# Matrix product with layer norm: a bank filled in another order, gamma and beta loaded at another place, their second copies cut finer

## The chip, the cores and the metric

The kernel runs on one core of a Trainium2 chip. TensorE multiplies matrices into PSUM, which has eight banks of 128 x 512 fp32 values; VectorE (DVE) and ScalarE (ACT) cast, copy and normalise; GpSimd (POOL) helps at the end; SyncE (SP) computes nothing and issues the DMA transfers between device memory and SBUF. The metric is the time on the device in microseconds, lower is better, as the median of several runs.

## The reference

```python
m, k, n = 2048, 2048, 2048          # all fp32, eps = 1e-5
x = np.matmul(a, b)
mean = np.mean(x, axis=-1, keepdims=True)
var = np.var(x, axis=-1, keepdims=True)
normalized = (x - mean) / np.sqrt(var + eps)
return (gamma * normalized + beta).astype(np.float32)
```

## The kernel before

Both matrices are cast to fp16 and multiplied with fp32 sums. The 2048 rows of `a` are 16 tiles of 128 rows; the inner dimension is 16 k-tiles of 128; the columns are four quarters of 512, one PSUM bank each. A tile's product is four quarters of 16 matmuls.

The first four tiles are worked on together while `b` comes in, k-tile by k-tile: the left half of the columns for k-tiles 0 to 3, the right half for k-tiles 0 to 7, then the rest. These products take seven banks, and the eighth serves the transposes of `a` on TensorE. The eighth product of each pass, the late bank, can only begin when the last transposes have been copied out of it. The right pass reads:

```python
early, late = right[:-1], right[-1]
for g, q in early:
    bank(g, q)
turns = {(1, 6): K1, (2, 4): K1 + 1, (3, 1): K1 + 2, (3, 5): K1 + 3}   # K1, K2 = 4, 8
for t in range(K1):
    if 0 < t < K1 - 1:
        cast_right(t + 1)              # half on VectorE, half on ScalarE
    for j, (g, q) in enumerate(early):
        mm(g, q, t, 0, K2)
        if (t, j) in turns:
            n = turns[t, j]
            turn_first(n)              # four transposes into the eighth bank
            keep_first(n)              # VectorE copies them out
            if n < 2 * K1 - 1:
                cast_first(n + 1)
cast_right(K1)
bank(*late)
for t in range(K1):
    mm(*late, t, 0, K2)
for t in range(K1, K2 - 1):
    cast_right(t + 1)
    for g, q in early:
        mm(g, q, t, 0, K2)
# ... the eighth k-tile, and the copies out of the banks ...
```

From tile 4 on the tiles of `a` are loaded in pieces of 64 KB (twenty transfers for a tile, in two halves), cast by ScalarE and transposed by VectorE. A tile's load, its cast, its transposes and its products are in different steps of the program:

```python
for t in range(K2, n_kt):
    load_b(t, 1)
for h in (0, 1):
    load_tile(4, h)                    # p_0 and p_1 in the profile
for h in (0, 1):
    load_tile(5, h)
# ... the products of the first four tiles ...
new_at(5)
for h in (0, 1):
    load_tile(6, h)
nc.sync.dma_start(gamma_b, gamma.unsqueeze(0).to_broadcast([P, N]))
nc.sync.dma_start(beta_b, beta.unsqueeze(0).to_broadcast([P, N]))
for c in range(4):
    if c % 2 == 0:
        cast_tile(5, c // 2)
        load_tile(7, c // 2)
    transpose_part(5, c)

for i in range(G, last):               # tiles 4 to 14
    if i > G:
        normalise(i - 1)
    if i == last - 2:
        load_halves()
    # ...
    for q in range(n_nb):
        bank(i, q)                     # eight banks in turn: tile 6 takes those of tile 4
        for t in range(n_kt):
            mm(i, q, t)
        stats(i, q)
        if i + 2 < n_mt:
            if q % 2 == 0:
                cast_tile(i + 2, q // 2)
                if i + 4 < n_mt:
                    load_tile(i + 4, q // 2)
            transpose_part(i + 2, q)
        # ...
        if q == 3 and i < 3 * G:
            normalise((i - G) // 2, (i - G) % 2)   # half of one of the first four tiles
```

`normalise` works on VectorE. Its first step for a quarter, `centre`, reads the bank, subtracts the mean and multiplies by `gamma_b`, and so frees the bank; its second, `scale`, multiplies by the inverse deviation and adds `beta_b`; then SyncE stores a half of the tile.

```python
def centre(i, q, u):
    nc.vector.scalar_tensor_tensor(
        u, x_of[i, q], mv_of[i][:, 0:1], gamma_b[:, ds(q * NB, NB)],
        AluOp.subtract, AluOp.mult)

def scale(i, q, u, c):
    nc.vector.scalar_tensor_tensor(
        c[:, ds(q % 2 * NB, NB)], u, rs_of[i], beta_b[:, ds(q * NB, NB)],
        AluOp.mult, AluOp.add)
```

The last tile is worked on as two blocks of 64 rows, each with its left columns on partitions 0 to 63 and its right columns on 64 to 127. It needs gamma and beta laid out in the same way, the second copies:

```python
def load_halves():
    for name, v in (("g", gamma), ("b", beta)):
        gb2[name] = bigp.tile([P, NH], FP32, tag="big", name=f"{name}2")
        for c in (0, 1):
            nc.sync.dma_start(
                gb2[name][ds(HR * c, HR), :],          # HR = 64, NH = 1024
                v[ds(c * NH, NH)].unsqueeze(0).to_broadcast([HR, NH]))
```

Every transfer reports its landing on one of eight semaphores, which are taken in turn (0 to 7), and waits for the transfer that had the same semaphore before it. The last four stores, of the second block of 64 rows, are issued by SyncE and ScalarE, two each.

Of the kernel before, what the change touches and what calls it, by code (L numbers as in the profile page):

```python
# [15 lines left out]
def kernel(  # L16
# [19 lines left out]
    nc = tc.nc  # L36
    P = 128
    M, K = a.shape
    _, N = b.shape
# [4 lines left out]
    NH = N // 2  # L44
# [15 lines left out]
    gamma_b = konst.tile([P, N], FP32)  # L60
    beta_b = konst.tile([P, N], FP32)
# [27 lines left out]
    def cast_right(kt, copies=(nc.vector.tensor_copy, nc.scalar.copy)):  # L89
        w = b_in.pop((kt, 1))  # L90
        for half, copy in enumerate(copies):
            copy(b16[:, kt, 1, ds(PAD + half * NB, NB)], w[:, ts(half, NB)])
# [17 lines left out]
    def cast_first(n):  # L110
        h = first16.tile([P, 4 * P], FP16, tag="h", name=f"h{n}")
        copy = nc.scalar.copy if n in (1, 3, 6, 7) else nc.vector.tensor_copy
        copy(h, a_in[n])
        a_in[n] = h

    def turn_first(n):
        t_of[n] = psum.tile([P, 4, P], FP16, tag="c_ps", bufs=8, name=f"t_ps{n}")
        if n >= 4:
            by_t = a_in[n].rearrange("m (p t) -> m t p", t=4)
        for j in range(4):  # L120
            if n < 4:
                by_t = a_in[n][:, ts(j // 2, 2 * P)].rearrange("m (p t) -> m t p", t=2)
            nc.tensor.transpose(t_of[n][:, j, :], by_t[:, j if n >= 4 else j % 2, :], ident)

    def keep_first(n):
        if n >= 4:
            g, c = pieces[n]
            nc.vector.tensor_copy(at[g][:, ds(4 * c, 4), :], t_of[n])
        else:
            g, e = 2 * (n % 2), n // 2  # L130
            nc.vector.tensor_copy(at[g][:, ts(e, 2), :], t_of[n][:, 0:2, :])  # L131
            nc.vector.tensor_copy(at[g + 1][:, ts(e, 2), :], t_of[n][:, 2:4, :])

    def load_tile(i, h):
        f = firstp.tile([P, 2, 4, P], FP32, tag="first", name=f"p{i}_{h}")
        for c in (0, 1):
            for q in range(4):
                to = f[ds(32 * q, 32), c]
                if h == 0 and c == 0:
                    for e in (0, 1):  # L140
                        nc.sync.dma_start(  # L141
                            to[:, :, ts(e, 64)], a_pieces0[q, e][:, ds(4 * i, 4)])
                else:
                    nc.sync.dma_start(to, a_pieces[q, 2 * h + c][:, ds(4 * i, 4)])  # L144
        tile_in[i, h] = f
# [21 lines left out]
    def bank(i, q):  # L167
        x_of[i, q] = psum.tile([P, NB], FP32, tag="c_ps", bufs=8, name=f"ps_{i}_{q}")

    def mm(i, q, kt, lo=0, hi=n_kt):  # L170
        nc.tensor.matmul(  # L171
            x_of[i, q], at[i][:, kt, :], b16[:, kt, q // 2, ds(PAD + q % 2 * NB, NB)],
            start=(kt == lo), stop=(kt == hi - 1),
        )
# [68 lines left out]
    HR = P // 2  # L243
    gb2, mean_parts = {}, {}
# [14 lines left out]
    def load_halves():  # L259
        for name, v in (("g", gamma), ("b", beta)):  # L260
            gb2[name] = bigp.tile([P, NH], FP32, tag="big", name=f"{name}2")
            for c in (0, 1):
                nc.sync.dma_start(
                    gb2[name][ds(HR * c, HR), :],
                    v[ds(c * NH, NH)].unsqueeze(0).to_broadcast([HR, NH]))

    def halves(name, lo, w):
        return gb2[name][:, ds(lo, w)]
# [131 lines left out]
    with tc.manual_schedule(engines=order):  # L400
# [13 lines left out]
        K1, K2 = 4, 8  # L414
# [19 lines left out]
            load_b(t, 1)  # L434
        for h in (0, 1):
            load_tile(4, h)
        for h in (0, 1):
            load_tile(5, h)

# [2 lines left out]
        early, late = left[:-1], left[-1]  # L442
# [52 lines left out]
        early, late = right[:-1], right[-1]  # L495
# [3 lines left out]
# [5 lines that stand above are left out]
                if (t, j) in turns:  # L504
                    n = turns[t, j]
                    turn_first(n)
                    keep_first(n)
                    if n < 2 * K1 - 1:
                        cast_first(n + 1)
        cast_right(K1)  # L510
        bank(*late)
        for t in range(K1):
            mm(*late, t, 0, K2)
        for t in range(K1, K2 - 1):
            cast_right(t + 1)
            for g, q in early:
                mm(g, q, t, 0, K2)
        for j, (g, q) in enumerate(early):
            mm(g, q, K2 - 1, 0, K2)
# [10 lines left out]
        early, late = left[:-1], left[-1]  # L530
        for g, q in early:
            bank(g, q)
        for t in range(K1, n_kt - 3):
            n = K1 + t
# [48 lines left out]
        new_at(5)  # L583
        for h in (0, 1):
            load_tile(6, h)
        nc.sync.dma_start(gamma_b, gamma.unsqueeze(0).to_broadcast([P, N]))
        nc.sync.dma_start(beta_b, beta.unsqueeze(0).to_broadcast([P, N]))
        for c in range(4):
            if c % 2 == 0:
                cast_tile(5, c // 2)  # L590
# [3 lines left out]
        for i in range(G, last):  # L594
            if i == 6:
                junk = xpool.tile([P, 2 * NB], FP16, tag="x_sb", name="junk")
# [4 lines that stand above are left out]
            if i == last - 1:  # L601
                mean_b()
            if i + 2 < n_mt:
                new_at(i + 2)
            for q in range(n_nb):
                bank(i, q)
# [9 lines that stand above are left out]
                if 6 <= i < 14:  # L616
                    sum_b(4 * (i - 6) + q, junk)
                if q == 3 and i < 3 * G:
                    normalise((i - G) // 2, (i - G) % 2)
# [33 lines left out]
```

## Time and profile before

| | before |
|---|---|
| time, median of 3 runs | 242.94 us (242.8 to 243.04) |
| span of the profiled execution | 242.0 us |
| TensorE busy | 232.4 us, 96% |
| VectorE busy | 196.2 us, 81% |
| ScalarE busy | 97.2 us, 40% |
| mean granted TensorE clock | 0.994 |
| moved by DMA | 53.71 MB, mean 222 GB/s |
| gamma_b, beta_b: issue to landing | 4.5 us, 7.3 us |

All times within the span are in microseconds from its first instruction. A line of a timeline has the start, the duration, the engine, the line of the kernel (L and a number), the operation, what it writes and what it reads, the shapes and the number of instructions merged; in brackets how long the engine stood idle before it and what ended that. A line of a list of waits has who waited for whom, the microseconds in total, how often, and the longest. SPq is SyncE's queue of DMA issues; the duration of an issue is that of the issuing instruction, not of the transfer. PEld is TensorE's load of weights. The numbers behind names only tell tiles of the same name apart: `at_708`, `at_819` and `at_874` are the transposed tiles 4, 5 and 6, and `p_0_216` and `p_1_229` are the two halves of tile 5, `p_0_820` and `p_1_833` those of tile 6, `p_0_846` the first half of tile 7.

### The profile page before, as it was taken

The numbers are of one execution on the slowest core, as the hardware profiler recorded it, in microseconds if no ns is written. First come the engines' busy times: TensorE is split into PE (matmuls) and PEld (weight loads), VectorE is DVE, ScalarE is ACT, GpSimd is POOL, SyncE is SP. The second block draws the span as 40 slices with busy tenths as digits, with TensorE's granted clock in tenths as the row PEclk, the third lists the DMA queues.
The fourth block names the chain that finished last, engine by engine and source line by source line (L and its number), as shares of the span: only waits on it lengthen the run. The fifth ranks groups of instructions, "written<-read, shape, count | busy, mean of one in ns | idle before, by whom it ended". The sixth has DMA issues, their size and how long they took to land.

```text
span 242.0 us, 3619 instructions
## 1 busy us (share of the span) xinstructions
PE 232.4 (96%) x1232; PEld 109.6 (45%) x1232; DVE 196.2 (81%) x377; ACT 97.2 (40%) x159; POOL 6.3 (3%) x10
## 2 busy tenths in 40 slices
PE   8999999999999999999999999999999999999970
PEld 2444455444444444444444444444444444444660
DVE  1476286588679477999999999999999999975882
ACT  3365353464112240219165645637190927301211
POOL 0000000000000000000000000000000000001241
PEclk9999999999999999999999999999999999999997
DMA  6999999994425385448475665648474847980433
GB/s 202 352 405 407 400 402 404 405 412 125 132 65 129 106 307 171 111 106 303 113 257 153 224 192 187 231 126 299 122 294 104 289 120 263 349 260 0 175 86 88
DMA packets 47569, 53.71 MB, mean 222 GB/s; under 512 B 17600, under 2 KB 37184, under 8 KB 47296
## 3 DMA queue, kind: packets, MB, share of 16 engines
q1 hardware_dynamic: 47392, 53.24, 65.4%
q10 hardware_dynamic: 160, 0.26, 0.3%
q8 instruction: 9, 0.15, 0.3%
q14 instruction: 8, 0.07, 0.1%
HBM read 36.70 MB, written 16.78 MB: 221 GB/s over the span
## 4 chain that ended last, share of the span: by engine, by line
issue 61%; DMA 24%; SPq 11%; POOL 1%; POOLq 0%; ACT 0%
SPq L144 6%; DMA w_1_192<-in_b_dram 4%; DMA f_2_144<-in_a_dram 4%; DMA w_0_176<-in_b_dram 4%; DMA w_0_118<-in_b_dram 4%; SPq L141 4%; DMA f_3_158<-in_a_dram 3%; DMA f_1_131<-in_a_dram 3%; DMA gamma_b<-in_gamma_dram 2%; SPq L106 1%; SPq L81 1%; POOL c_0_2529 L316 1%; POOL c_1_2306 L316 1%; POOLq L648 0%; ACT b_93 L87 0%
## 5 line engine op out<-in xcount | busy, mean ns | idle before, releaser
L248 ACT ACTIVATE junk<-b_93 128x1024 f16<-128x1024 f16 x32 | 33.7, 1054 | 0.5
L274 PEld LDWEIGHTS <-at_2109 128*64 128x64 f16 x192 | 9.9, 110 | 4.5 <-issue 0.4
L171 PEld LDWEIGHTS <-at_874 128*128 128x128 f16 x64 | 6.3, 98 | 8.3 <-issue 0.9
L171 PEld LDWEIGHTS <-at_819 128*128 128x128 f16 x64 | 6.3, 98 | 7.5
L171 PEld LDWEIGHTS <-at_1431 128*128 128x128 f16 x64 | 6.3, 98 | 7.5
L171 PEld LDWEIGHTS <-at_1995 128*128 128x128 f16 x64 | 6.3, 98 | 7.5
L171 PEld LDWEIGHTS <-at_1149 128*128 128x128 f16 x64 | 6.3, 98 | 7.5
L171 PEld LDWEIGHTS <-at_1293 128*128 128x128 f16 x64 | 6.3, 98 | 7.5
L171 PEld LDWEIGHTS <-at_1713 128*128 128x128 f16 x64 | 6.3, 98 | 7.5
L171 PEld LDWEIGHTS <-at_1857 128*128 128x128 f16 x64 | 6.3, 98 | 7.5
L171 PEld LDWEIGHTS <-at_708 128*128 128x128 f16 x64 | 6.3, 98 | 7.6
L171 PEld LDWEIGHTS <-at_1014 128*128 128x128 f16 x64 | 6.2, 97 | 7.6
L171 PEld LDWEIGHTS <-at_1575 128*128 128x128 f16 x64 | 6.2, 97 | 7.6
L171 PEld LDWEIGHTS <-at_238 128*128 128x128 f16 x64 | 6.1, 98 | 7.7 <-DVE at_238 L131 0.5
L171 PEld LDWEIGHTS <-at_239 128*128 128x128 f16 x64 | 6.2, 98 | 7.1
L171 PEld LDWEIGHTS <-at_241 128*128 128x128 f16 x64 | 6.2, 98 | 6.7 <-issue 0.6
L171 PEld LDWEIGHTS <-at_240 128*128 128x128 f16 x64 | 6.1, 98 | 6.5 <-DVE at_240 L131 0.4
L408 PE MATMUL w_ps<-warm 128*128 128x512 f16 x16 | 6.7, 601 | 1.2 <-DVE warm L401 1.2
L312 POOL TENSOR_TENSOR u_3_2300<-u_3_2300,gamma_b 128x512 f32<-128x512 f32 x1 | 1.3, 1276 | 221.2 <-ACT u_3_2300 L311 221.2
L248 ACT ACTIVATION_READ_ACCUMULATOR junk<-b_93 128x1 f32 x32 | 6.0, 187 | 0.0
L408 PEld LDWEIGHTS <-warm 128*128 128x128 f16 x16 | 2.2, 144 | 4.8 <-issue 3.6
L171 PE MATMUL ps_1_501<-b_93,at_239 128*128 128x512 f16 x12 | 4.2, 379 | 0.0
(576 smaller groups left out, 560.7 us busy)
## 6 DMA issues: line engine op xcount, KB each, us to landing
gamma_b<-in_gamma_dram SPq DMA_DIRECT2D x1, 1024.0 KB, 4.5
beta_b<-in_beta_dram SPq DMA_DIRECT2D x1, 1024.0 KB, 7.3
w_0_106<-in_b_dram SPq DMA_DIRECT2D x1, 512.0 KB, 4.3
f_0_108<-in_a_dram SPq DMA_DIRECT2D x2, 256.0 KB, 4.7
w_0_111<-in_b_dram SPq DMA_DIRECT2D x1, 512.0 KB, 6.6
f_0_113<-in_a_dram SPq DMA_DIRECT2D x2, 256.0 KB, 7.4
w_0_116<-in_b_dram SPq DMA_DIRECT2D x1, 512.0 KB, 8.0
w_0_118<-in_b_dram SPq DMA_DIRECT2D x1, 512.0 KB, 8.7
```

The lines of the kernel that those rows point to most:

```text
L81: (queue or nc.sync).dma_start(w, rows[:, ds(h * NH, NH)])
L106: nc.sync.dma_start(a_in[n].rearrange("p (g k) -> p g k", g=2), a[ts(n % 2, 2 * P), ts(n // 2, 2 * P)].rearrange("(g p) k -> p g k", p=P))
L141: nc.sync.dma_start(to[:, :, ts(e, 64)], a_pieces0[q, e][:, ds(4 * i, 4)])
L144: nc.sync.dma_start(to, a_pieces[q, 2 * h + c][:, ds(4 * i, 4)])
L171: nc.tensor.matmul(x_of[i, q], at[i][:, kt, :], b16[:, kt, q // 2, ds(PAD + q % 2 * NB, NB)], start=(kt == lo), stop=(kt == hi - 1),)
L248: nc.scalar.activation(junk, b16[:, kt, h, ds(PAD, NH)], ActFn.Copy, accum_out=b_sum[:, h, kt:kt + 1])
L274: nc.tensor.matmul(x[ds(HR * c, HR), 0:w], at[last][:, t, ds(HR * b, HR)], b16[:, t, c, ds(PAD + lo, w)], start=(t == 0), stop=(t == n_kt ...
L312: nc.gpsimd.tensor_tensor(u, u, g, AluOp.mult)
L316: nc.gpsimd.tensor_tensor(o, u, b, AluOp.add)
L408: nc.tensor.matmul(w_ps, warm[:, 0:P], warm, start=True, stop=True)
```

## The change

There are three parts. In the right pass of the first four tiles, products of the fifth k-tile (number 4) are put between the last transposes and the late bank's first products, so that TensorE has work while the bank is being copied out; the cast of that k-tile moves ahead of the copy. `gamma_b` and `beta_b` are loaded between tiles 4 and 5, instead of after tile 6, so that they are there before they are first wanted. The second copies of gamma and beta are loaded by eight transfers of 32 partitions instead of four of 64; the transfers after them, the last stores among them, then use semaphores four further on (4 to 7 for the last four stores).

```diff
     def load_halves():
         for name, v in (("g", gamma), ("b", beta)):
             gb2[name] = bigp.tile([P, NH], FP32, tag="big", name=f"{name}2")
-            for c in (0, 1):
+            for p in range(4):
                 nc.sync.dma_start(
-                    gb2[name][ds(HR * c, HR), :],
-                    v[ds(c * NH, NH)].unsqueeze(0).to_broadcast([HR, NH]))
+                    gb2[name][ds(32 * p, 32), :],
+                    v[ds(p // 2 * NH, NH)].unsqueeze(0).to_broadcast([32, NH]))
@@
         for h in (0, 1):
             load_tile(4, h)
+        nc.sync.dma_start(gamma_b, gamma.unsqueeze(0).to_broadcast([P, N]))
+        nc.sync.dma_start(beta_b, beta.unsqueeze(0).to_broadcast([P, N]))
         for h in (0, 1):
             load_tile(5, h)
@@
                 if (t, j) in turns:
                     n = turns[t, j]
                     turn_first(n)
+                    if n == 2 * K1 - 1:
+                        cast_right(K1)
                     keep_first(n)
                     if n < 2 * K1 - 1:
                         cast_first(n + 1)
-        cast_right(K1)
-        bank(*late)
-        for t in range(K1):
-            mm(*late, t, 0, K2)
         for t in range(K1, K2 - 1):
             cast_right(t + 1)
-            for g, q in early:
+            for j, (g, q) in enumerate(early):
+                if (t, j) == (K1, 3):
+                    bank(*late)
+                    for u in range(K1):
+                        mm(*late, u, 0, K2)
                 mm(g, q, t, 0, K2)
@@
         for h in (0, 1):
             load_tile(6, h)
-        nc.sync.dma_start(gamma_b, gamma.unsqueeze(0).to_broadcast([P, N]))
-        nc.sync.dma_start(beta_b, beta.unsqueeze(0).to_broadcast([P, N]))
```

## The prediction

> **What bounds the kernel now.** I read the page's busy line and its 40 slices first, then who waited for whom, then the timelines of the engines around each place where TensorE waits.
>
> ```profile
> PE 232.4 (96%) x1232; PEld 109.6 (45%) x1232; DVE 196.2 (81%) x377; ACT 97.2 (40%) x159; POOL 6.3 (3%) x10
> PE   8999999999999999999999999999999999999970
> ```
>
> TensorE is busy 96% of the span, at a granted clock of 0.994. From 96 us to the last tile its groups of 16 products start 3.45 us apart without a gap, 216 ns for a product. So only two things count: TensorE's few pauses, and the tail after its last product. Its list of waits names the pauses:
>
> ```profile
> PE ps_0_1150 L171 <- DVE u_0_997 L207: 0.6, 1, 0.6
> PE ps_3_435 L171 <- DVE at_241 L128: 0.3, 1, 0.3
> ```
>
> A matmul is shown 380 ns long because ends are modelled, so what a pause costs is read from starts. The late bank (ps_3_435) first:
>
> ```profile
> 22.17 0.42 DVE L128 COPY at_240<-t_ps_414 128x512 f16<-128x512 f16 x1 [0.66 <-PE t_ps_414 L123]
> 22.37 0.62 ACT L92 CAST b_93<-w_1_134 128x512 f16<-128x512 f32 x1 [0.58 <-DMA w_1_134<-in_b_dram]
> 23.06 0.38 PE L171 MATMUL ps_2_370<-b_93,at_241 128*128 128x512 f16 x1
> 23.26 0.42 DVE L128 COPY at_241<-t_ps_426 128x512 f16<-128x512 f16 x1 [0.66 <-PE t_ps_426 L123]
> 23.74 1.02 PE L171 MATMUL ps_3_435<-b_93,at_241 128*128 128x512 f16 x4 [0.30 <-DVE at_241 L128]
> ```
>
> 23.74 − 23.06 − 0.216 = **0.46 us** lost: the bank is free only when VectorE has copied the last transposes out of it. The second pause, with what VectorE did before it:
>
> ```profile
> 88.90 0.71 DVE L162 STREAM_TRANSPOSE at_874<-a_1_947 128x512 f16<-128x512 f16 x1 [1.36 <-ACT a_1_947 L149]
> ...
> 93.83 0.75 DVE L213 SCALAR_TENSOR_TENSOR c_0_982<-u_0_983,rs_985,beta_b 128x512 f32<-128x512 f32 x1 [1.37 <-DMA beta_b<-in_beta_dram]
> 95.45 0.75 DVE L207 SCALAR_TENSOR_TENSOR u_0_997<-ps_0_875,mv_992,gamma_b 128x512 f32<-128x512 f32 x1
> 96.25 3.61 PE L171 MATMUL ps_0_1150<-b_93,at_874 128*128 128x512 f16 x16 [0.57 <-DVE u_0_997 L207]
> ```
>
> The group before starts at 92.06, so 92.06 + 16 × 0.216 = 95.52 was possible: **0.73 us** lost. Tile 6 takes the bank of tile 4, which is free 0.80 us after VectorE starts to centre tile 4 (95.45 to 96.25). The reader should see two waits of VectorE ahead of that: 1.37 us for beta, and 1.36 us for ScalarE's cast of tile 6, which itself waits for its loads. Those are SyncE's:
>
> ```profile
> 87.82 1.04 ACT L149 CAST a_1_947<-p_1_833 128x1024 f16<-128x1024 f32 x1 [2.80 <-DMA p_1_833<-in_a_dram]
> 65.62 5.13 SPq L141 DMA_DIRECT2D p_0_216<-in_a_dram  x8
> 70.80 1.85 SPq L144 DMA_DIRECT2D p_0_216<-in_a_dram  x4
> 72.69 3.75 SPq L144 DMA_DIRECT2D p_1_229<-in_a_dram  x8
> 76.55 3.69 SPq L141 DMA_DIRECT2D p_0_820<-in_a_dram  x8
> 80.28 1.85 SPq L144 DMA_DIRECT2D p_0_820<-in_a_dram  x4
> 82.24 3.69 SPq L144 DMA_DIRECT2D p_1_833<-in_a_dram  x8
> 85.98 0.43 SPq L586 DMA_DIRECT2D gamma_b<-in_gamma_dram  x1
> 86.45 0.43 SPq L587 DMA_DIRECT2D beta_b<-in_beta_dram  x1
> 86.98 7.08 SPq L141 DMA_DIRECT2D p_0_846<-in_a_dram  x8
> ```
>
> SyncE issues one transfer per 0.475 us without a pause: tile 5 (p_0_216, p_1_229), tile 6 (p_0_820, p_1_833), gamma, beta, tile 7 (p_0_846). The last block of eight takes 7.08 us instead of 3.69: an issue waits until the transfer eight before it has landed. Its eighth starts at 93.8, when beta has landed (86.45 + 7.3), and SyncE's list of waits has it:
>
> ```profile
> SPq L141 <- DMA beta_b<-in_beta_dram: 2.8, 1, 2.8
> ```
>
> **What the Trainium skill says.** "Perfetto Trace Analysis", What "DMA-bound" means, counts as its second kind an issuing sequencer whose track is solid with DMA slices: the trace agrees, SyncE's track is solid from 65.6 to 101 us while the DMA engines are 52% busy from 66 to 96. The same page, DMA Instruction — HWDGE, says the profiled issue leaves out the movement of the data: the trace agrees, 0.43 us of issue against 2.1 us to landing for a tile's pieces and 7.3 for beta. "TensorE: Matmul & The Clock Gate", Back-to-back issue gap, gives about 131 ns for 512 columns in a stream of loads and products; the trace has 216, and I use that.
>
> **The change part by part.**
>
> (1) Late bank. After the product at 23.06 come three products of the fifth k-tile (0.65 us) and only then the late bank's four. They need the fifth k-tile's cast: ScalarE's half runs 22.37 to 22.99; VectorE's moves ahead of the copy at 23.26 and fits between 22.51 and 22.93. So they start at 23.28, the late bank at 23.93, when the copy (done 23.74) is over. Nothing is added; 0.46 us goes. Later casts of this stage have slack: the eighth k-tile is cast by 28.12 and wanted at 28.68, the last left one is begun on at 48.25 (VectorE done 48.67) and wanted at 48.87. But part of the gain is taken at tile 4: VectorE transposes its second half from 68.50 (ready about 69.2), behind loads paced by SyncE, and TensorE loads those weights at 69.40. Only 0.16 to 0.25 us is free there, so I carry some 0.2 us on to 81 us.
>
> (2) Gamma and beta sooner. Removed: the 1.37 us wait of VectorE. Added: both transfers now stand in SyncE's queue ahead of tiles 5 and 6. Without them, the first half of tile 5 takes from 65.62 to 72.69 = 7.07 us; with them, tile 7's first half took from 85.98 to 96.06 = 10.08 us. The delay is 10.08 − 7.07 = **3.01 us** for everything behind. (One issue of tile 5 alone lasts 1.81 us by the view of line L141; I take it to fall inside the wait for beta.) Tile 5 bears this: its last weights are transposed about 83.6 and wanted near 83.9; the third quarter is ready near 82.95 and wanted near 83.0, so it is close. Tile 6 doesn't: its cast moves from 87.82 to 90.83, and VectorE, which takes its orders in sequence, begins to centre tile 4 at 95.45 + 3.01 − 1.37 = 97.09. The bank is free at 97.89 instead of 96.25: **1.64 us later**. TensorE's gain from (1) doesn't matter, for it only waits longer: from about 95.3 to 97.9, some 2.6 us by starts. Afterwards both engines keep their distance and nothing gives it back.
>
> (3) Second copies by 32 partitions. Four issues (2 of 1.32 us and 2 of 0.61 at 206 to 210.5) become eight of half the size. By the pace of this stage they end at 211 to 213; the store behind them waits for VectorE until 211.5 anyway, and the copies are read from 229 on. Cost zero. The four transfers more shift by four which of the eight semaphores the last stores use. At the end SyncE runs through its semaphores in waits: the line for the kernel's end has seven waits from 240.6 to 242.0, of which four cheap ones (some 0.066 us apart) follow the last landing. With the last stores on the later semaphores two or three of these come before the landing: **0.15 us** saved.
>
> Sum: 242.94 + 1.64 − 0.15 = 244.43.
>
> **Rivals.** (a) Both pauses go as intended: −0.46 − 0.73 − 0.15, 241.6 us. For it: both waits are real and lie on TensorE. Against: it needs tile 6's loads to stay where they are, and the 7.08 us block shows what a queue with beta in it does. With a delay of at most 1.37 + 0.26 us this rival would come out near the old time. (b) The same mechanism, but the 1.81 us issue isn't absorbed, and one like it falls behind tile 5: 1.4 us more, 245.8. (c) Tile 5 becomes a wait of its own: its third quarter misses TensorE at 83.0 by some tenths. That would only move waiting from tile 6 to tile 5, the end being set by tile 6: same total. (d) The DMA engines are freer at 66 us than at 86 and beta lands sooner, say after 5.5 us: the delay is then 1.2 us, and the time 242.6.
>
> **Range and chances.** The delay of 3.01 us is the term that decides; I leave it 1.5 to 4 us, which gives 242.9 to 245.4. Centre 244.4. A 2% change would be 4.86 us, more than any rival makes: faster 0.01, same 0.97, slower 0.02.
>
> **What would show it.** Right: gamma_b issued near 65.6; the issue that waits for beta now in p_0_216, near 73.4; the cast of p_1_833 near 90.8 instead of 87.82; no more DVE wait for beta_b; the wait of PE for u_0_997 at about 2.4 us (0.6 before); ps_3_435 without a wait at 24; a short wait of PEld at tile 4's third quarter. Wrong: a cast of p_1_833 before 89.4 us (then the queue lets gamma and beta pass), or TensorE starting tile 6 by 95.5 us.

## The result, and the profile after

The kernel after takes **245.69 us** (244.76 to 247.32, 5 runs) against 242.94 us before (242.61 to 243.04, 5 runs on the same chip): a ratio of 1.0124, 95% interval 1.0082 to 1.0165. The change costs some 2.8 us, about twice what was expected.

The page of the kernel after, its busy line and its slices of TensorE:

```profile
PE 230.9 (95%) x1232; PEld 108.9 (45%) x1232; DVE 196.0 (80%) x377; ACT 97.0 (40%) x159; POOL 6.3 (3%) x10
PE   7899999999999896899999999999999999999980
```

A dent has come in the slices 14 to 17 (79 to 104 us). TensorE's list of waits, after, names what is in it (the 1.2 us at the warm-up, `w_ps`, stands in both kernels):

```profile
PE ps_0_1150 L171 <- DVE u_0_997 L207: 2.5, 1, 2.5
PE w_ps L408 <- DVE warm L401: 1.2, 1, 1.2
PE ps_0_1015 L171 <- DVE at_821 L162: 1.0, 1, 1.0
```

The late bank is gone from the list; tile 6's wait for tile 4's bank has grown from 0.6 to 2.5 us; tile 5's wait for its own transposes (`at_821`) is new. TensorE's timeline, after, gives them by starts:

```profile
22.86 0.38 PE L171 MATMUL ps_2_368<-b_93,at_241 128*128 128x512 f16 x1
23.07 1.03 PE L171 MATMUL ps_3_442<-b_93,at_243 128*128 128x512 f16 x4
23.94 0.38 PE L171 MATMUL ps_3_369<-b_93,at_241 128*128 128x512 f16 x1
...
80.39 1.89 PE L171 MATMUL ps_0_1015<-b_93,at_821 128*128 128x512 f16 x8
83.28 1.90 PE L171 MATMUL ps_0_1015<-b_93,at_821 128*128 128x512 f16 x8 [0.99 <-DVE at_821 L162]
...
91.92 3.62 PE L171 MATMUL ps_3_1099<-b_93,at_821 128*128 128x512 f16 x16
98.08 3.62 PE L171 MATMUL ps_0_1150<-b_93,at_874 128*128 128x512 f16 x16 [2.54 <-DVE u_0_997 L207]
```

The late bank's four products (ps_3_442) start 0.21 us after the product before them: its pause of 0.46 us is removed. Tile 5 stands for 83.28 − 80.39 − 8 × 0.216 = 1.16 us, tile 6 for 98.08 − 91.92 − 16 × 0.216 = 2.70 us. SyncE's timeline, after, has the cause:

```profile
64.49 0.43 SPq L437 DMA_DIRECT2D gamma_b<-in_gamma_dram  x1
64.97 0.43 SPq L438 DMA_DIRECT2D beta_b<-in_beta_dram  x1
65.44 8.62 SPq L141 DMA_DIRECT2D p_0_218<-in_a_dram  x8
74.11 1.86 SPq L144 DMA_DIRECT2D p_0_218<-in_a_dram  x4
76.01 3.75 SPq L144 DMA_DIRECT2D p_1_231<-in_a_dram  x8
...
85.55 3.70 SPq L144 DMA_DIRECT2D p_1_835<-in_a_dram  x8
```

The block of eight behind beta takes 8.62 us, where the one behind beta before took 7.08. Its list of waits says for what:

```profile
SPq L141 <- DMA beta_b<-in_beta_dram: 4.2, 1, 4.2
```

And the page, after, has the two transfers, whose last column is microseconds from issue to landing:

```profile
gamma_b<-in_gamma_dram SPq DMA_DIRECT2D x1, 1024.0 KB, 4.7
beta_b<-in_beta_dram SPq DMA_DIRECT2D x1, 1024.0 KB, 8.8
```

Beta takes 8.8 us instead of 7.3. What follows from it, in the timelines of ScalarE and VectorE after:

```profile
91.11 1.04 ACT L149 CAST a_1_947<-p_1_835 128x1024 f16<-128x1024 f32 x1 [2.79 <-DMA p_0_846<-in_a_dram]
```

```profile
95.66 0.75 DVE L213 SCALAR_TENSOR_TENSOR c_0_982<-u_0_983,rs_985,beta_b 128x512 f32<-128x512 f32 x1
97.28 0.75 DVE L207 SCALAR_TENSOR_TENSOR u_0_997<-ps_0_875,mv_992,gamma_b 128x512 f32<-128x512 f32 x1
```

(The cast needs p_1_835; that a transfer of the next tile is named in its brackets is an inference of the profile.) VectorE's wait for beta is gone, as meant. To compare with the profile before, the two must be lined up: the execution profiled before was some 1.1 us behind already when tile 4 was loaded (it took 243.8 us, more than any of the five that give the median). I take the first issue behind tile 4's as zero, 65.62 before and 64.49 after:

| from the first issue behind tile 4 | before | after | difference |
|---|---|---|---|
| tile 6's second cast (87.82; 91.11) | 22.20 | 26.62 | +4.42 |
| TensorE starts tile 6 (96.25; 98.08) | 30.63 | 33.59 | +2.96 |
| end of the span (242.03; 243.66) | 176.41 | 179.17 | +2.76 |

All of the loss is there when tile 6 starts. 4.42 less VectorE's removed wait of 1.37 is 3.05, near the 2.96; from tile 6 to the end both take the same, less 0.20 us, nearly all of it in the tail.

### The profile page after: what moved, and what is told of

Read it like the earlier page. It is cut to its first block, busy times and chain, and to the rows that moved or that the text cites. A ratio compares the mean times of both kernels' runs of the same rounds, so it can differ in the third digit from the quotient of the medians.

```text
span 243.7 us, 3623 instructions
## 1 busy us (share of the span) xinstructions
PE 230.9 (95%) x1232; PEld 108.9 (45%) x1232; DVE 196.0 (80%) x377; ACT 97.0 (40%) x159; POOL 6.3 (3%) x10
## 4 chain that ended last, share of the span: by engine, by line
PE 54%; DMA 26%; SPq 10%; issue 3%; DVE 3%; ACT 1%; POOL 1%; POOLq 0%; DVEq 0%
SPq L144 6%; DMA f_2_144<-in_a_dram 4%; DMA w_1_192<-in_b_dram 4%; DMA w_0_176<-in_b_dram 4%; DMA beta_b<-in_beta_dram 4%; DMA f_3_158<-in_a_dram 3%; DMA f_1_131<-in_a_dram 3%; DMA w_0_118<-in_b_dram 3%; SPq L141 2%; PE ps_0_1150 L171 1%; PE ps_last_0_2323 L274 1%; PE ps_last_1_2356 L274 1%; PE ps_3_2179 L171 1%; PE ps_3_2061 L171 1%; PE ps_1_2019 L171 1%
## 5 line engine op out<-in xcount | busy, mean ns | idle before, releaser
L408 PE MATMUL w_ps<-warm 128*128 128x512 f16 x16 | 5.2, 486 | 1.2 <-DVE warm L401 1.2
L171 PE MATMUL ps_0_1150<-b_93,at_874 128*128 128x512 f16 x16 | 3.6, 379 | 2.5 <-DVE u_0_997 L207 2.5
L149 ACT CAST a_0_844<-p_0_218 128x1024 f16<-128x1024 f32 x1 | 1.0, 1046 | 10.8 <-DMA p_1_231<-in_a_dram 10.8
```

The lines of the kernel that those rows point to most:

```text
L149: nc.scalar.copy(a16, tile_in.pop((i, h)))
L171: nc.tensor.matmul(x_of[i, q], at[i][:, kt, :], b16[:, kt, q // 2, ds(PAD + q % 2 * NB, NB)], start=(kt == lo), stop=(kt == hi - 1),)
L408: nc.tensor.matmul(w_ps, warm[:, 0:P], warm, start=True, stop=True)
```

## The experiments

All have the kernel before on the same chip beside them: 242.67 us for the first four, 242.83 for the next four, 242.87 for the last two. In their profiles names carry no numbers. "Delay" is that of tile 6's second cast against before, lined up on the landing of the last piece of `b`: the cast starts 28.28 us after that landing before and 32.68 in the kernel after, which gives 4.40 us. A pause of TensorE is taken from starts.

### Gamma and beta alone

The late bank and the second copies as before; only the two lines for `gamma_b` and `beta_b` are moved.

```diff
             load_tile(4, h)
+        nc.sync.dma_start(gamma_b, gamma.unsqueeze(0).to_broadcast([P, N]))
+        nc.sync.dma_start(beta_b, beta.unsqueeze(0).to_broadcast([P, N]))
         for h in (0, 1):
             load_tile(5, h)
@@
-        nc.sync.dma_start(gamma_b, gamma.unsqueeze(0).to_broadcast([P, N]))
-        nc.sync.dma_start(beta_b, beta.unsqueeze(0).to_broadcast([P, N]))
```

> Gamma and beta sooner alone, late bank and second copies as before. Theory (queue): SyncE's queue is held until beta has landed, tile 6 comes some 4.4 us later in the profile of the change, VectorE's old wait for beta (1.37 us) goes, so TensorE starts tile 6 about 2.9 us later relative to the end of b's loads; the late bank's 0.46 us is swallowed by that wait. So 245.7 to 246.0 us, with PE waiting 2 us or more for u_0_997. Rival (the parts interact, the late bank's new order is what costs): well under 245 us here.

Measured: 246.46 us (245.33 to 248.45), ratio 1.016 (1.0123 to 1.0197), above the 245.7 to 246.0 that were expected. Gamma and beta landed after 5.1 and 9.2 us, the delay was 5.08 us. The move alone gives the whole loss and more; the late bank's new order isn't what costs. In its timeline of TensorE something more stands behind tile 6's pause:

```profile
98.74 13.49 PE L171 MATMUL ps<-b,at 128*128 128x512 f16 x55 [2.55 <-DVE u L207]
```

55 products have 54 steps from start to start, 54 × 0.216 = 11.66 us, and the last is shown 0.38 long: 12.04. They took 13.49, so 1.45 us more was lost after the pause. The windows of this kernel (the length of the stretch, busy time of PE, PEld, DVE, ACT and POOL, then the granted clock, the DMA share, GB/s) say how:

```profile
97.00:99.00 2.00, 0.26 (x1) 0.10 (x1) 1.96 (x6) 1.05 (x2) 0.00 (x0) 0.82 0.58 116
99.00:101.00 2.00, 2.00 (x6) 0.73 (x5) 2.00 (x4) 0.29 (x1) 0.00 (x0) 0.50 0.56 155
101.00:103.00 2.00, 2.00 (x10) 0.76 (x8) 2.00 (x4) 0.56 (x1) 0.00 (x0) 0.82 0.25 51
```

TensorE's granted clock falls to half for some 3 us after the pause. The profiled execution of the kernel after doesn't show this (its group of 16 at 98.08 lasts 3.62 us as always, mean clock 0.992), but the longest of its five runs, 247.32 us, has a mean clock of 0.986, where the other four have 0.992 to 0.994. So the pause has two prices, its own length and sometimes a slow restart.

### Late bank and copies, gamma and beta in their old place

```diff
-        nc.sync.dma_start(gamma_b, gamma.unsqueeze(0).to_broadcast([P, N]))   # behind tile 4
-        nc.sync.dma_start(beta_b, beta.unsqueeze(0).to_broadcast([P, N]))
@@
         for h in (0, 1):
             load_tile(6, h)
+        nc.sync.dma_start(gamma_b, gamma.unsqueeze(0).to_broadcast([P, N]))
+        nc.sync.dma_start(beta_b, beta.unsqueeze(0).to_broadcast([P, N]))
```

> Late bank and second copies as changed, gamma and beta back at their old place. Theory (queue): TensorE still waits for tile 4's bank until VectorE has had beta, and VectorE is set by tile 6's loads, not by TensorE, so the 0.46 us of the late bank turns into a longer wait for u_0_997 (0.57 to about 0.7 to 1.0 us); only the tail's 0.13 us stays: 242.8 us. Rival (the late bank's gain counts in full): 242.3 us. Rival (the late bank's order costs something): over 243.2 us.

Measured: 242.35 us (241.93 to 243.36), ratio 0.9989 (0.9975 to 1.0004). The late bank's pause is gone, and its list of waits of TensorE has tile 6 instead:

```profile
PE ps L171 <- DVE u L207: 0.9, 1, 0.9
```

By starts this pause is 1.09 us where it was 0.73. In this execution, then, 0.36 of the 0.46 us that the late bank gave is waited away in front of tile 4's bank; it is the longest of the kernel's runs, so take the size as rough. The median gain of 0.3 us lies between the theory's 0.13 and the rival's 0.6, but it is hardly more than that of the copies alone, which come next: so the medians too leave little to the late bank, 0.07 us and less than the noise.

### The copies alone

The kernel before, with `load_halves` by 32 partitions and nothing else.

> Only the second copies by 32 partitions, so that the last stores use the semaphores 4 to 7. Theory: 0.13 to 0.15 us less in the waits after the last landing, 242.8 us, and no other trace of it. Rival (eight issues instead of four hold the stores of tile 13 and reach the end): 243.2 us or more. Rival (the order of semaphores doesn't matter): 242.94 us.

Measured: 242.42 us (242.11 to 242.84), ratio 0.9988 (0.9978 to 0.9998), some 0.25 us less. Four issues more, and no loss by them. From the last store's landing to the end of the span it is 0.89 us here and in the kernel after, 1.08 before and 1.07 with gamma and beta alone: the 0.19 us less goes with the cut of the copies, at the place that the expectation names. In its profiled execution tile 6 has no pause at all, though its loads stand in the same order as before: what TensorE loses there varies from one execution to the next.

### Gamma and beta behind tile 6 as column halves

If a transfer of 1 MB holds the queue, smaller ones in the old place might not. (Against the change; its two lines behind tile 4 are gone.)

```diff
         for h in (0, 1):
             load_tile(6, h)
+        for h in (0, 1):
+            for to, v in ((gamma_b, gamma), (beta_b, beta)):
+                nc.sync.dma_start(
+                    to[:, ds(h * NH, NH)],
+                    v[ds(h * NH, NH)].unsqueeze(0).to_broadcast([P, NH]))
```

> As the change, but gamma and beta stay behind tile 6 and come in two halves of 1024 columns each, in the order gamma left, beta left, gamma right, beta right. Theory (queue): nothing is put ahead of tile 6, and beta's left half lands after 1 MB instead of 2, about 90.5 us instead of 93.7, before VectorE wants it at 92.4; so VectorE's wait of 1.37 us goes, tile 4's bank is free at about 94.9 us, and TensorE goes on without the pause of 0.73 us, plus some 0.2 us from the late bank and 0.13 from the tail: 241.6 to 241.9 us. Rival (the left half of beta doesn't land sooner, since the pieces share the engines): 242.8 us.

Measured: 243.22 us (242.12 to 244.52), ratio 1.0025 (1.0012 to 1.0038): missed. Tile 6's pause is gone, and the same pause has come one tile later. TensorE's timeline and SyncE's:

```profile
93.64 15.05 PE L171 MATMUL ps<-b,at 128*128 128x512 f16 x69
110.07 6.21 PE L171 MATMUL ps<-b,at 128*128 128x512 f16 x28 [1.38 <-DVE u L207]
```

```profile
86.61 8.21 SPq L141 DMA_DIRECT2D p<-in_a_dram  x8
```

The four halves hold tile 7's loads for 8.21 us; its cast comes 3.0 us later than before (41.32 instead of 38.30 after `b`'s last piece), and TensorE stands 1.54 us at tile 7. What stands behind these bytes in the one queue comes late; the place chooses which tile that is, and so whether TensorE has to wait for it.

### Gamma and beta between the halves of tile 5

```diff
+        load_tile(5, 0)
         nc.sync.dma_start(gamma_b, gamma.unsqueeze(0).to_broadcast([P, N]))
         nc.sync.dma_start(beta_b, beta.unsqueeze(0).to_broadcast([P, N]))
-        for h in (0, 1):
-            load_tile(5, h)
+        load_tile(5, 1)
```

> As the change, but gamma and beta stand between the two halves of tile 5. Theory (queue, and an instruction fetch of 16 KB that fell into beta's transfer at 69.7 us and made it land after 8.8 us instead of 7.3): the transfers now run at about 71 to 77 us, behind that fetch, so beta lands after some 7.3 us, tile 6 is some 3.0 us late instead of 4.4, and the time is 1.5 us over the kernel before: 244.2 us. Rival (beta is slow at this place of the program whatever the fetch): 8.8 us to landing and 245.5 us, as the change.

Measured: 247.6 us (245.71 to 248.53), ratio 1.0177 (1.0144 to 1.0211): missed, on the far side. Tile 5's first eight issues took 5.09 us, as before, and beta still landed only after 8.5 us. So here the slow issue and the slow landing both came, the two things that the prediction had let fall together; the delay was 5.60 us. TensorE stood 1.63 us at tile 5 and 2.76 at tile 6. The landing is nearly the rival's, and no fetch of 16 KB lies in this transfer: by the records that the section on fetches uses they lie at 66.8 and 100.7 us (one of 8 KB lies in it, at 77.1). Beta was late in another way here, without a straggler: 15 to 21 packets are under way from 73.5 to 80.5 us. Some were slow, 36 of the pair's 256 packets of 8 KB took over 0.45 us, where 0.31 is the median; but so did 33 in the kernel with late bank and copies, where beta landed after 7.3 us. Why it was late is not known.

### Four pieces, spread singly over tiles 5 and 6

```diff
-        nc.sync.dma_start(gamma_b, gamma.unsqueeze(0).to_broadcast([P, N]))
-        nc.sync.dma_start(beta_b, beta.unsqueeze(0).to_broadcast([P, N]))
-        for h in (0, 1):
-            load_tile(5, h)
+        piece(gamma_b, gamma, 0)      # a column half each
+        load_tile(5, 0)
+        piece(beta_b, beta, 0)
+        load_tile(5, 1)
+        piece(gamma_b, gamma, 1)
@@
-        for h in (0, 1):
-            load_tile(6, h)
+        load_tile(6, 0)
+        piece(beta_b, beta, 1)
+        load_tile(6, 1)
```

> As the change, but gamma and beta come in four pieces of 1024 columns, spread singly over the loads of tiles 5 and 6. Theory (it is the wait for a landing that holds SyncE, not the bytes): each piece lands before the issue eight places later, so it costs only its own issue, 4 x 0.475 = 1.9 us for tile 6 less VectorE's 1.37 us: 0.5 us later at tile 6, 243.0 us. Rival (the bytes themselves hold tile 6's loads): 3 us or more late as in the change, 245 us.

Measured: 246.26 us (243.87 to 247.44), ratio 1.0125 (1.009 to 1.0161): missed. The pieces landed after 5.25, 4.11, 4.16 and 4.80 us; eight issues behind them take 3.8. So each piece still held the queue for the rest, by the list of SyncE's waits:

```profile
SPq L144 <- DMA beta_b<-in_beta_dram: 1.4, 2, 1.0
SPq L141 <- DMA gamma_b<-in_gamma_dram: 1.1, 2, 0.7
```

The delay is 3.25 us (expected 1.9), the pause at tile 6 is 2.74 us, and five of the six runs have the slow restart (mean clock 0.985 to 0.987); the sixth, with 0.993, took 243.87 us.

### The instruction fetches moved

What makes beta land 1.5 us later than before? In the trace's records of transfers a fetch of 16 KB of instructions (the page's queue "q8 instruction", nine such in a run) lies on one DMA engine at 69.7 us after, in the middle of beta's flood. Before, the fetch of that place lies at 67.6, at the very issue of tile 5 that takes 1.81 us, and the next at 98.0, at another of 1.40 us. The two issues stand out in the views of lines L141 and L144, before (durations in ns: shortest, median, longest):

```profile
L141 SPq DMA_DIRECT2D p_0_216<-in_a_dram x8: 430/430/1807, 65.6 to 70.3; - x8
L144 SPq DMA_DIRECT2D p_1_863<-in_a_dram x8: 376/430/1397, 96.1 to 100.3; - x8
```

After, the windows show a lone straggler:

```profile
71.00:72.00 1.00, 1.00 (x7) 0.41 (x5) 1.00 (x3) 0.00 (x0) 0.00 (x0) 1.00 1.03 232
72.00:73.00 1.00, 1.00 (x6) 0.47 (x5) 1.00 (x3) 0.00 (x0) 0.00 (x0) 1.00 0.12 24
73.00:74.00 1.00, 1.00 (x7) 0.47 (x5) 1.00 (x3) 0.00 (x0) 0.00 (x0) 1.00 0.07 14
```

Until 72 us the 16 DMA engines are all busy (share 1.03), from then to 73.7, when beta lands, nearly idle (0.12, 0.07): sixteenths of a share, so one engine or two have work left. The records of transfers agree: while the fetch runs (69.66 to 70.60), 15 packets of data are under way on average instead of 16, and from 72.5 to 73.7 just one. In the two profiles with such a fetch in the transfer (after; gamma and beta alone) beta landed after 8.8 and 9.2 us, in six without one after 7.15 to 7.84; the kernel between the halves, 8.5 without one, is the exception. The fetches seem to come in step with TensorE's instructions. So 16 warm-up products were made into 48 narrow ones, to bring the fetch forward.

```diff
-            for _ in range(n):
-                nc.tensor.matmul(w_ps, warm[:, 0:P], warm, start=True, stop=True)
+            for _ in range(3 * n):
+                nc.tensor.matmul(w_ps[:, 0:171], warm[:, 0:P], warm[:, 0:171],
+                                 start=True, stop=True)
```

> The change with its 16 warm-up products cut into 48 of a third of the width, so that TensorE's instructions are the same from there on but each later fetch of instructions comes some 7 us sooner (near 63 us instead of 69.7). Theory (the fetch in beta's transfer made it slow): beta lands after about 7.3 us instead of 8.8, tile 6 is 3.0 us late instead of 4.4, and the time is 1.4 us below the change's: 244.1 us. Rival (the fetch is harmless): 8.8 us, and the change's 245.5 us.

Measured: 247.52 us (246.26 to 248.0), ratio 1.0182 (1.0158 to 1.0207). The time missed; the mechanism is half borne out. The fetches did follow TensorE's instructions, though by some 11 us and not 7. They moved to 58.8 and 86.7, out of beta's flood, and beta landed after 7.1 us, not 8.8. But SyncE's timeline has lost it elsewhere:

```profile
58.66 6.60 SPq L144 DMA_DIRECT2D p<-in_a_dram  x12
...
66.26 7.00 SPq L141 DMA_DIRECT2D p<-in_a_dram  x8
...
83.04 6.38 SPq L144 DMA_DIRECT2D p<-in_a_dram  x12
```

The block behind beta takes 7.00 us, as before (8.62 after). The two blocks of twelve in which the fetches now fall take 6.60 and 6.38 instead of 5.65. In sum the delay is 4.70 us: two fetches now fall on SyncE's chain ahead of tile 6 instead of one, they cost it 0.95 and 0.73 us, and moving them gained nothing. TensorE stood 3.35 us at tile 6, and all runs have the slow restart.

### Left columns behind tile 6, right columns later

Against the change; its two lines behind tile 4 are gone.

```diff
+        columns(0)                     # gamma and beta, left half, behind load_tile(6, h)
         for c in range(4):
             if c % 2 == 0:
                 cast_tile(5, c // 2)
                 load_tile(7, c // 2)
+                if c == 0:
+                    columns(1)     # their right half
```

> A version meant to beat both: late bank and second copies as changed; gamma's and beta's left columns behind tile 6, their right columns between the halves of tile 7. Theory: tile 6 isn't delayed, VectorE's wait for beta goes or is under 0.5 us, and tile 7's second half comes no later than before, so that neither tile 6 (0.73 us before) nor tile 7 (1.54 us with all four pieces behind tile 6) is waited for: 1.0 to 1.3 us under the kernel before, 241.4 to 241.7 us. Rival (tile 7 is still late): 242.5 us or more.

Measured: 242.67 us (241.52 to 244.07), ratio 0.9997 (0.9981 to 1.0013): missed. Tile 6 doesn't wait, but TensorE stands 2.04 us at tile 7: beta's right half landed after 7.38 us, with a fetch at 95.7 in it, and held tile 7's second half, in SyncE's list of waits:

```profile
SPq L144 <- DMA beta_b<-in_beta_dram: 2.4, 1, 2.4
```

This execution is the longest of 22 (244.07 us), so 2.04 us is not the usual pause; the shortest took 241.52 us, as had been expected.

In each profile of a new order of the one queue TensorE is left with a pause, at tile 5, 6 or 7. So the next kernel takes loads out of that queue.

### Half of tiles 5 and 6 issued by ScalarE

The late bank and the copies of the change; gamma and beta behind tile 6; the second halves of tiles 5 and 6 are issued by ScalarE between its casts.

```diff
-    def load_tile(i, h):
+    def load_tile(i, h, queue=None):       # issues on queue, SyncE if None
@@
-        for h in (0, 1):
-            load_tile(5, h)
+        load_tile(5, 0)
@@ behind cast_tile(4, 1)
+        load_tile(5, 1, nc.scalar)
@@
-            load_tile(6, h)
+        load_tile(6, 0)
@@ behind cast_tile(5, 1)
+        load_tile(6, 1, nc.scalar)
+        # then gamma_b, beta_b, and tile 7 on SyncE
```

> A version meant to beat both: late bank and second copies as changed, gamma and beta behind tile 6, but the second halves of tiles 5 and 6 (sixteen of SyncE's issues) are issued by ScalarE, right after its casts of tiles 4 and 5. Theory (SyncE's one issue per 0.475 us is what sets tile 6, and so TensorE): tile 6's cast comes 2 to 3 us sooner than before, beta lands before VectorE wants it, neither tile 6 nor tile 7 is waited for, and now the late bank's 0.46 us counts too: 1.0 to 1.3 us under the kernel before, 241.4 to 241.8 us. Rival (the transfers, not their issue, set tile 6): no better than 242.4 us.

Measured: **242.16 us** (241.59 to 242.56), ratio 0.9968 (0.9955 to 0.998): less than both kernels, though by 0.7 us and not the 1.0 to 1.3 expected. Tile 6's second cast comes 5.2 us sooner than before. Its list of TensorE's waits from 0.2 us on:

```profile
PE w_ps L409 <- DVE warm L402: 1.2, 1, 1.2
PE ps L172 <- DVE b L86: 0.5, 1, 0.5
PE ps L172 <- DVE at L131: 0.2, 1, 0.2
```

All three are of the first 25 us; no wait is left at tiles 4 to 7. Yet beta lands after 7.3 us here too, and SyncE waits for it, as its timeline and ScalarE's show:

```profile
78.85 0.35 SPq L594 DMA_DIRECT2D gamma_b<-in_gamma_dram  x1
79.24 0.43 SPq L595 DMA_DIRECT2D beta_b<-in_beta_dram  x1
79.78 7.06 SPq L142 DMA_DIRECT2D p<-in_a_dram  x8
```

```profile
66.46 5.41 ACTq L145 DMA_DIRECT2D p<-in_a_dram  x8
...
75.55 3.32 ACTq L145 DMA_DIRECT2D p<-in_a_dram  x6
80.72 1.99 ACT L150 CAST a<-p 128x1024 f16<-128x1024 f32 x2 [4.21 <-DMA p<-in_a_dram]
```

SyncE has sixteen issues fewer ahead of gamma and beta, so the pair goes out 6 us sooner than before (20.2 us after the landing of `b`'s last piece instead of 26.4), and tile 7, behind it, has that much time in hand when beta takes it. "DMA: Bandwidth & Descriptors", Issuing engines are not separate DMA queues, in the Trainium skill says that issuing from several engines saves only the issuing sequencer's time, which is "usually small relative to the DMA itself". The trace agrees that this is what is saved, but here it isn't small: sixteen issues by 0.475 us are 7.6 us of a queue that is solid from 65 to 100 us.

### The same with the late bank's old order

The kernel just shown, with the right pass of the first four tiles as it was before.

> The same without the late bank's new order. Theory (the late bank's gain is real but was swallowed by TensorE's wait for tile 4's bank): without that wait it shows, this is 0.4 to 0.5 us slower than the version with it, 241.9 to 242.2 us. Rival (the late bank's order brings nothing): the same time as the version with it.

Measured: 242.48 us (242.19 to 242.88), ratio 0.9981 (0.9971 to 0.9991). Of the pauses from the late bank on, the late bank's own is back in its profile, and no other. So with tile 6's wait gone the late bank's new order seems to be worth about 0.3 us of its 0.46; the intervals of the two ratios overlap (0.9955 to 0.998, 0.9971 to 0.9991), so this is likely and not shown.

## Why the prediction was wrong by 1.3 us

Its mechanism stands; one term of its sum was too small.

**The late bank (1)** went as worked out: 0.46 us less, nothing added. That the gain doesn't reach the end fits the medians too, but the place differs: in the profile with this part and the copies alone, tile 4's weights cost 0.07 us only, and 0.36 us is waited away at tile 6.

**Gamma and beta (2)** is the step that failed: "the delay is 10.08 − 7.07 = 3.01 us". From gamma's issue to the end of tile 5's first half it was 76.01 − 64.49 = 11.52 us, so 11.52 − 7.07 = 4.45. The prediction took SyncE's block of tile 5 with its 1.81 us issue as the time without gamma and beta, took tile 7's block as the time with them, and so let the slow issue "fall inside the wait for beta". The cause of that issue, an instruction fetch on the same DMA engines, didn't vanish: it fell into beta's transfer and lengthened the wait itself, 8.76 us to landing instead of 7.28, **1.48 us**. The 7.07 us had such a fetch in them (tile 5's first eight issues take 5.13 us where tile 6's take 3.69, 1.44 more), the 10.08 had none; with a fetch in both, as both kernels have one there, the working gives 10.08 + 1.44 − 7.07 = 4.45. Put 4.40 for 3.01 in its sum: 242.94 + 4.40 − 1.37 − 0.15 = 245.82, against 245.69 measured. Rival (b), 245.8, had the size, and nearly the cause.

With the slow restart the same sum holds for every kernel that has gamma and beta ahead of tile 6:

| kernel | delay | slow restart | base + delay − 1.37 − 0.15 + restart | its profiled execution |
|---|---|---|---|---|
| after | 4.40 | none | 245.82 | 245.43 |
| gamma and beta alone (no copies: no 0.15) | 5.08 | 1.45 | 247.83 | 247.54 |
| between the halves of tile 5 | 5.60 | 1.65 | 248.56 | 248.53 |
| four pieces, spread | 3.25 | 1.68 | 246.24 | 246.34 |
| fetches moved | 4.70 | 1.33 | 247.34 | 246.96 |

The restart is worked out for each as in the first experiment, the base is the median of the kernel before on the same chip; all five come within 0.4 us. That supports the chain: queue, cast, VectorE's order of work, bank, TensorE, end.

**Tile 5 (rival c)** did become a wait, 1.16 us, and by the chain above changed nothing in the total, as that rival said: tile 6's start sets the end. **The tail (3)** went as worked out: 0.19 us less from the last landing to the end; 0.15 was said. **The signs** came in number and kind: gamma issued at 64.49 (65.62 on the old scale), no wait for beta on VectorE, 2.5 us for u_0_997; the cast of tile 6 at 91.11 (92.24 on the old scale) instead of near 90.8 carries the error. The short wait of TensorE's weight load at tile 4 came as well: 0.18 us at 68.16, for the second half's transposes, without a pause of the products. Rivals (a) and (d) fell: nothing of the queue's wait was spared at 65 us.

**The range** left the delay up to 4 us. It was drawn about the one number, not from what it rested on: one landing time, seen once, beside a stray long issue of unknown cause.

What stays open: why a fetch of 16 KB, about 1 us on one DMA engine, takes 0.6 to 1.9 us of SyncE's chain. That they coincide, and move together, is shown; how one delays the other is not. Also why beta is as slow between the halves of tile 5 without such a fetch. Of the 1.3 us that the kernel with ScalarE's issues could gain (pauses of 0.46 and 0.73 us, 0.15 of the tail), its profiled execution has 1.1 from TensorE's first product to the end of the span (232.8 us against 233.9): near 12 us, where TensorE stood 0.13 us before, it stands 0.45, the 0.5 of its list. The medians show 0.7; that the 0.73 isn't there in every execution of the kernel before, as the profile of the copies alone suggests, may be the rest, and was not measured.

## What to carry to other kernels

Where one queue issues everything in order and semaphores are taken in turn, a large transfer among small ones holds those behind it until it has landed; moving it sooner moves the wait to whatever now stands behind it. What removed the wait here was to take issues out of that queue. Reckon what is behind the large transfer, not only who wants its data. An unexplained long issue in a chain that you shift is a cost that will come again: don't subtract it as absorbed before its cause is known.

## What the runs showed of the hardware

- **A slow restart.** After pauses of 2.7 to 3.4 us TensorE's granted clock fell to half (0.50 in the windows) for some 3 us, which cost 1.3 to 1.7 us in four profiles; by the mean clock (0.984 to 0.988, where 0.989 and more is usual) it came in one of five runs of the kernel after and in all six of the kernel with the longest pause. "TensorE: Matmul & The Clock Gate", HAM oscillation, in the Trainium skill gives gaps of over some 3.4 us as what does this; here a pause of 2.71 us did it in one profile and one of 2.70 did not in another, and pauses of 1.5 to 2.0 us at tile 7 show no drop in the mean clock (0.994).
- **Instruction fetches lie on the data's DMA engines.** One of 16 KB came every 20 to 30 us in the kernel before, took 0.94 us at 69.7 in the kernel after, and each one that fell where SyncE issued without a pause (59 to 101 us) went with 0.6 to 1.9 us more of an issue or a landing. One of 8 KB, at 74.9 us before, left the eight issues around it at 3.75 us, as long as others.
- **Half a broadcast landed hardly sooner than a whole one.** Halves of 512 KB took 4.1 to 5.3 us when issued singly, where a whole megabyte took 4.5 to 5.4 as gamma, and 7.1 to 9.2 as beta right behind it: cutting them in two didn't halve the time that the queue is held.
